# Sparse-attention layer of a two-block network: the value products of both attention branches issued together per tile of queries, and the compressed probabilities transposed at full width

## The chip, the cores and the metric

The kernel runs on one core of a Trainium2 chip. The metric is the device time of one execution in microseconds; lower is better. The engines are TensorE (PE, with its weight loads shown apart as PEld), VectorE (DVE), ScalarE (ACT), GpSimd (POOL) and the DMA queue of SyncE (SP).

## The reference, cut to what matters

The program is two two-layer blocks on 512 tokens of width 1024. Only the last mixer, the sparse attention (NSA), is touched by the change:

```
q = rope(q.reshape(B, S, 16, 64)) * 64 ** -0.5          # 4 groups of 4 heads share keys and values
kcmp, vcmp = compress(kc), compress(vc)                  # 31 compressed keys and values
block of queries:
    pc = softmax(where(valid, q @ kcmp, NEG));  o_c = pc @ vcmp
    ps = softmax(where(causal, q @ k_sel, NEG)); o_s = ps @ v_sel   # 8 blocks of 64, top 16: all are selected
    pw = softmax(where(window, q @ kwin, NEG)); o_w = pw @ vwin      # window 512 = the sequence
o = sum over the three of gates * out;  o = o * silu(z);  y = o @ w_out
```

With 512 tokens every block is selected and the window covers everything, so the second and third softmax are full causal attention with keys and values of their own.

## The kernel before, in words

The heads are worked in 8 pairs p of 2 heads j; a pair has 4 tiles t of 128 queries. One (p, t) is a *unit*; there are 32. A unit has two branches b. Branch 0 holds the compressed and the selected attention, branch 1 the window. `probs` issues the scores of one branch of a unit on TensorE (lines 1741, 1746, 1748 for b = 0, line 1752 for b = 1), takes the maximum and the exponentials on VectorE and ScalarE (lines 1757 and 1763), and multiplies the probabilities by gate and reciprocal sum on VectorE (line 1771).

`attend` goes through the units. For each branch it transposes the probabilities `p` of both heads on TensorE (line 1803), copies them on ScalarE from PSUM to a tile `at` (line 1805), and for b = 0 also transposes the compressed probabilities `pc` (line 1808) and copies them on VectorE to `pcT` (line 1809). It then issues the same branch's scores of the *next* unit (`first(u + 1, b)`) and last the value products into the accumulator `po` (line 1815 with the compressed values `vcz`, line 1818 with `vs`). A product has 64 output columns in its weights, so that head 0 writes partitions 0 to 63 and head 1 partitions 64 to 127; all other matmuls of this stage are 128 wide. A float32 product is two passes in the trace, so a pair of them (j = 0 and 1) is four rows.

The order of the work comes from two things. `attend` is a generator, and the main stream (the projections of z, of the next group's queries and keys, and then the output projection, all recorded by lines 225 to 227) calls `tick` between its matmuls; `tick` steps every generator whose due time has passed. A `yield cost, latency` sets the next due time, with `LT = LA = 0.36` and `LQ = 0`. Behind that, the build lays the instructions of each engine in an order of its own and gives the PSUM tiles `sm` (4 buffers, for scores and transposes) and the SBUF tiles their places, so the final order is seen only in the built program. `finish` multiplies the accumulator by z (line 1829) when a pair is done; the output projection waits for it.

Of the kernel before, what the change touches and what calls it, by code (L numbers as in the profile page):

```python
# [16 lines left out]
P = 128  # L17
# [4 lines left out]
LQ, LT, LA = 0.0, 0.36, 0.36  # L22
# [83 lines left out]
class Net:  # L106
# [1416 lines left out]
    def nsa_(self, x, after):  # L1523
        nc, a = self.nc, self.a
        V, G, S = nc.vector, nc.gpsimd, nc.scalar
        mm, tr = nc.tensor.matmul, nc.tensor.transpose
        ident, w = self.ident, a["nsa_w_in_2"][0]
        one = lambda shape, name, dt=F32: self.wk.tile(shape, dt, name=name, tag=name, bufs=1)
        s2 = lambda tag, bufs, shape=(P, T), dt=F32: self.t(list(shape), tag, bufs, dt)
# [54 lines left out]
        vcz = one([P, 4, 2, 64], "vcz")  # L1584
# [3 lines left out]
        m = P - 1  # L1588

        def small(i):  # L1590

            n = "kv"[i]
            tmp = s2("p", 4)
            per = tmp[:16, 384:]
            nc.sync.dma_start(per, a[f"nsa_pe_{n}_2"][0].rearrange("(i s) d -> i (s d)", s=2))
            pp = self.sm_ps()
            tr(pp[:, :16], per, ident[:16, :16])
            pe = s2("pe", 2, (P, 16))
            V.tensor_copy(pe, pp[:, :16])
            w2 = tmp[:, :256].rearrange("p (k j c) -> p k j c", k=2, j=2)  # L1600
            for j in range(2):
                nc.sync.dma_start(w2[:, :, j], a[f"nsa_c{n}_w2_2"][0].rearrange("(k p) c -> p k c", p=P))
            pes[i] = pe, w2, tmp[:, 256:]

        def prepare(i, b):

            if b == 0:
                small(i)
            while not all(by_t[i, t].done for t in range(NT)):
                yield 0.0, 0.5  # L1610
            src = flat[i].rearrange("p g c -> p (g c)")[:, 16 * b:16 * b + 16 * m]
            src = src.rearrange("p (c i e) -> p e i c", e=2, i=8)[:, 0]
            if (i, b) == (1, 0):
                hl = [s2("Q2", 4, (P, 2, T), F32R).rearrange("p j c -> p (j c)") for _ in range(2)]
            else:
                c8 = self.c8().rearrange("p (j i) c -> p j (i c)", j=2)
                hl = [c8[:, 0], c8[:, 1]]
            hl = [v.rearrange("p (i c) -> p i c", c=P)[:, :, :m] for v in hl]
            for c in range(0, 8, 4):
                raw = s2("at", 3).rearrange("p (i c) -> p i c", c=P)[:, :, :m]  # L1620
                k = 8 * b + c
                (G if i else V).tensor_tensor(raw, src[:, c:c + 4], pes[i][0][:, k:k + 4, None].to_broadcast([P, 4, m]),
                                              op=ALU.add)
                self.split(hl[0][:, c:c + 4], hl[1][:, c:c + 4], raw)
                yield 0.0, 1.2
            parts[i, b] = hl
# [94 lines left out]
        used = [Flag() for _ in range(8)]  # L1721
        pairs = [Flag() for _ in range(8)]
        pcT = [one([P, P], f"pcT{i}") for i in range(2)]
        for i in range(2):
            V.memset(pcT[i], 0.0)
        cat = [None, None]
        lhs = Operand(lambda k, s, n: [v[:, k % 4, s:s + n] for v in cat[k // 4]])
        zt = {}
# [45 lines left out]
        pp, pcs, pos = {}, {}, {}  # L1774

        def attend():
            units = [(p, t) for p in range(8) for t in range(NT)]

            def first(u, b):
                p, t = units[u]  # L1780
                if b == 0:
                    if t == 0:
                        while p // 2 not in grp or len(grp[p // 2]) < NT or not all(s.done for s in grp[p // 2].values()):
                            yield 0.0, 1.8
                    pcs[u] = s2("pc", 2, (P, 64)), s2("st", 3, (P, 2, 6))
                pp[u, b] = probs(p, b, t, *pcs[u])
                yield 0.0011 * 128 * (t + 1) + 0.3, LQ

            yield from first(0, 0)
            yield from first(0, 1)  # L1790
            yield 0.0, 0.8
            for u, (p, t) in enumerate(units):
                g = p // 2
                c = slice(t * P, (t + 1) * P)
                if t == 0:
                    pos[p] = self.mm_ps()
                po = pos[p]
                for b in range(2):
                    at = []
                    for j in range(2):  # L1800
                        pt = self.sm_ps()
                        for i in range(t + 1):
                            tr(pt[:, i * P:(i + 1) * P], pp[u, b][j][:, i * P:(i + 1) * P], ident)  # L1803
                        at.append(s2("at", 3))
                        S.copy(at[j][:, :(t + 1) * P], pt[:, :(t + 1) * P])
                    if b == 0:
                        pt = self.sm_ps()
                        tr(pt[:64, :P], pcs[u][0], ident)
                        V.tensor_copy(pcT[t % 2][:64], pt[:64, :P])
                    yield 0.22 * (t + 1), LT  # L1810
                    if u + 1 < len(units):
                        yield from first(u + 1, b)
                    if b == 0:
                        for j in range(2):
                            mm(po[j * 64:(j + 1) * 64, c], vcz[:, g, j], pcT[t % 2], start=True, stop=False)
                    for i in range(t + 1):
                        for j in range(2):
                            mm(po[j * 64:(j + 1) * 64, c], vs[g][:, i, b * 64:(b + 1) * 64],  # L1818
                               at[j][:, i * P:(i + 1) * P], start=False, stop=b == 1 and i == t)
                    yield 0.27 * (t + 1) + 0.13, LA  # L1820
                if t == NT - 1:
                    used[p].done = True
                    self.spawn(finish(p, po), 1.45)

        def finish(p, po):
            while p not in zt:
                yield 0.0, 0.5
            z = zt[p]
            V.tensor_tensor(z, z, po, op=ALU.mult)  # L1829
            if cat[p // 4] is None:  # L1830
                cat[p // 4] = (self.c8(), self.c8())
            self.split(cat[p // 4][0][:, p % 4], cat[p // 4][1][:, p % 4], z)
            pairs[p].done = True
            yield 0.0, 0.0
# [13 lines left out]

        self.lin_nat(x, w, 0, 8, [(1024, 256), (2560, 48)], ev_c(0))
        preps = [self.spawn(prepare(0, b), 2.0) for b in range(2)]  # L1850
        self.lin_nat(x, w, 0, 8, [(1280, 256)], ev_c(1))
        preps.append(self.spawn(prepare(1, 0), 2.0))
        group(0)
        compress(0, preps[:2], lambda: preps.append(self.spawn(prepare(1, 1))))
        compress(1, preps[2:])
        self.spawn(attend(), 6.0)
        for g in range(4):
            z_block(g)
# [64 lines left out]
```

## Time and profile before

| what | value |
|---|---|
| median of 3 runs | 1997.81 us (1997.23 to 1997.83) |
| the profiled execution: time, span | 1995.69 us, 1994.0 us |
| TensorE clock granted | 0.995 of full speed |
| TensorE busy | 1924.9 us, 97% of the span |
| VectorE, ScalarE, GpSimd busy | 1451.8, 1014.8, 217.0 us |
| transposes of p (line 1803) in the trace | 320, from 1675.8 to 1966.8 us |
| value products (line 1818) in the trace | 640 passes, from 1677.5 to 1968.7 us |

The units of attention run from about 1669 to 1970 us of the span. The form `128*64` in a row is a matmul with 64 columns of weights, `128*128` one with 128. In a timeline a row with `x8` is eight neighbouring instructions, with its start and the time to the last one's end. The duration of a single matmul includes its pipeline; what it costs TensorE is the step from its start to the next one's start.

### The profile page before, as it was taken

What the parts mean: (1) busy time and instruction counts of PE and PEld (TensorE: products, weight loads), DVE (VectorE), ACT (ScalarE), POOL (GpSimd) and SP (SyncE); (2) the same over time, 40 slices, a digit from 0 to 9 for tenths busy, and PEclk for the clock granted to TensorE, in tenths of its full rate; (3) what the DMA queues carried; (4) which work ended last, traced back from release to release, by engine and by line L of the source; (5) the groups of instructions that cost most, each with busy time, mean ns of one, the idle gap of its engine ahead of it and who ended that gap; (6) DMA issues with size and microseconds to landing.
All of it is one profiled execution on the core that took longest, in us unless ns stands there. A gap on an engine that the chain in (4) does not pass through costs nothing.

```text
span 1994.0 us, 29961 instructions
## 1 busy us (share of the span) xinstructions
PE 1924.9 (97%) x11221; PEld 1602.4 (80%) x11221; DVE 1451.8 (73%) x2823; ACT 1014.8 (51%) x2144; POOL 217.0 (11%) x213
## 2 busy tenths in 40 slices
PE   7989989999999999999999999999999999999997
PEld 7778769788796888877879788788888797777776
DVE  5876857887989465787878897945445687878866
ACT  4645244454465245666446365525433455666664
POOL 1121110000000031431000000000110131010100
PEclk9999999999999999999999999999999999999999
DMA  6212222334333122211422343212412235202101
GB/s 182 80 32 70 74 85 85 106 96 128 94 96 121 39 90 85 75 43 57 145 84 85 116 121 112 86 51 76 132 43 84 77 91 129 64 8 58 46 20 43
DMA packets 148066, 165.08 MB, mean 83 GB/s; under 512 B 29168, under 2 KB 105024, under 8 KB 147920
## 3 DMA queue, kind: packets, MB, share of 16 engines
q1 hardware_dynamic: 147920, 163.16, 27.5%
q8 instruction: 89, 1.46, 0.3%
q14 instruction: 57, 0.47, 0.1%
HBM read 161.03 MB, written 2.10 MB: 82 GB/s over the span
## 4 chain that ended last, share of the span: by engine, by line
PE 74%; DVE 14%; ACT 4%; POOL 3%; issue 3%; DMA 2%; SPq 0%; DVEq 0%; POOLq 0%; ACTq 0%
PE mm L225 17%; PE mm L226 17%; PE mm L227 17%; PE mm L463 5%; DVE wlo L184 3%; POOL ss L297 2%; PE mm L1818 2%; PE sm L314 2%; PE sm L1803 1%; PE sm L227 1%; PE sm L225 1%; PE sm L226 1%; DVE hn L351 1%; PE sm L1752 1%; ACT whi L183 1%
## 5 line engine op out<-in xcount | busy, mean ns | idle before, releaser
L184 DVE TENSOR_TENSOR wlo<-raw,whi 128x1024 fp32r<-128x1024 f32 (+4 forms) x223 | 267.2, 1204 | 89.0 <-ACT whi L183 85.7
L183 ACT CAST whi<-raw 128x1024 fp32r<-128x1024 f32 (+4 forms) x223 | 224.7, 1011 | 142.1 <-PE mm L226 64.7
L225 PE MATMUL mm<-whi,xh 128*128 128x512 f32 (+3 forms) x768 | 286.6, 374 | 1.2 <-ACT whi L183 1.2
L226 PE MATMUL mm<-wlo,xh 128*128 128x512 f32 (+3 forms) x768 | 276.2, 360 | 2.6 <-DVE wlo L184 2.5
L227 PE MATMUL mm<-whi,xl 128*128 128x512 f32 (+3 forms) x768 | 276.9, 361 | 1.2 <-DVE xl L319 1.2
L225 PE MATMUL mm<-whi,c 128*128 128x512 f32 (+1 forms) x536 | 219.5, 410 | 1.7 <-DVE zt L1829 0.8
L183 ACT CAST whi<-qr 128x1024 fp32r<-128x1024 f32 x108 | 112.8, 1050 | 186.5 <-PE mm L227 124.8
L227 PE MATMUL mm<-whi,c 128*128 128x512 f32 (+1 forms) x536 | 207.5, 388 | 0.0
L226 PE MATMUL mm<-wlo,c 128*128 128x512 f32 (+1 forms) x536 | 207.1, 387 | 0.3 <-DVE wlo L184 0.3
L225 PE MATMUL mm<-xh,whi 128*128 128x512 f32 (+1 forms) x480 | 172.2, 359 | 0.0
L226 PE MATMUL mm<-xl,whi 128*128 128x512 f32 (+1 forms) x480 | 167.5, 349 | 0.0
L227 PE MATMUL mm<-xh,wlo 128*128 128x512 f32 (+1 forms) x480 | 167.3, 348 | 0.0
L297 POOL TENSOR_TENSOR ss<-ss,mhalf 128x1 f32<-128x1 f32 (+2 forms) x56 | 59.7, 1065 | 981.4 <-DVE ss L296 981.0
L225 PEld LDWEIGHTS mm<-whi,xh 128*128 128x128 f32 x768 | 145.8, 190 | 23.7 <-issue 6.3
L226 PEld LDWEIGHTS mm<-wlo,xh 128*128 128x128 f32 x768 | 146.6, 191 | 20.9 <-DVE wlo L184 4.6
L227 PEld LDWEIGHTS mm<-whi,xl 128*128 128x128 f32 x768 | 145.8, 190 | 21.7 <-DVE xl L319 1.8
L184 DVE TENSOR_TENSOR wlo<-qr,whi 128x1024 fp32r<-128x1024 f32 x108 | 131.4, 1225 | 32.0 <-ACT whi L183 31.4
L225 PEld LDWEIGHTS mm<-whi,c 128*128 128x128 f32 (+1 forms) x536 | 101.0, 188 | 26.3 <-issue 5.7
L226 PEld LDWEIGHTS mm<-wlo,c 128*128 128x128 f32 (+1 forms) x536 | 101.0, 188 | 21.5 <-issue 3.8
L227 PEld LDWEIGHTS mm<-whi,c 128*128 128x128 f32 (+1 forms) x536 | 100.7, 188 | 20.4 <-DVE c L184 0.2
L225 PE MATMUL mm<-T,whi 128*128 128x256 f32 x384 | 108.8, 283 | 0.0
L227 PE MATMUL mm<-T,wlo 128*128 128x256 f32 x384 | 108.8, 283 | 0.0
(510 smaller groups left out, 4433.8 us busy)
## 6 DMA issues: line engine op xcount, KB each, us to landing
qr<-in_w_mlp SPq DMA_DIRECT2D x84, 512.0 KB, 4.1
raw<-in_w_mlp SPq DMA_DIRECT2D x44, 512.0 KB, 4.3
raw<-in_w_ple_gate SPq DMA_DIRECT2D x16, 512.0 KB, 4.1
raw<-in_w_qkv_o SPq DMA_DIRECT2D x32, 256.0 KB, 4.1
raw<-in_w_in_e SPq DMA_DIRECT2D x48, 128.0 KB, 2.9
raw<-in_nsa_w_in SPq DMA_DIRECT2D x10, 512.0 KB, 3.8
raw<-in_nsa_w_in SPq DMA_DIRECT2D x17, 256.0 KB, 3.1
raw<-in_w_in_e SPq DMA_DIRECT2D x8, 512.0 KB, 4.8
```

Source lines behind the costliest of these rows:

```text
L183: self.nc.scalar.copy(hi, src)
L184: self.nc.vector.tensor_tensor(lo, src, hi.bitcast(F32), op=ALU.subtract)
L225: mm(out, sh, mh, start=first, stop=False, **kw)
L226: mm(out, sh, ml, start=False, stop=False, **kw)
L227: mm(out, sl, mh, start=False, stop=last, **kw)
L297: self.pow = self.nc.gpsimd.tensor_tensor(ss, ss, self.mhalf[:, :n], op=ALU.pow)
L314: nc.tensor.transpose(ps[:, j * P:(j + 1) * P], src[:, (k + j) * P:(k + j + 1) * P], self.ident)
L351: nc.vector.scalar_tensor_tensor(hn, self.h[:, t, :], ss, own["g"], op0=ALU.mult, op1=ALU.mult)
L463: nc.tensor.matmul(pss[r], hops[s][:, 2 * c + k, r * P:(r + 1) * P], w[:, k], start=fresh and c == 0 and k == 0, stop=c == 1 and k == 1, s ...
L1752: mm(ps[:, :n], q, kt[2 + i][:, :n], start=i == 0, stop=i == 1)
L1803: tr(pt[:, i * P:(i + 1) * P], pp[u, b][j][:, i * P:(i + 1) * P], ident)
L1818: mm(po[j * 64:(j + 1) * 64, c], vs[g][:, i, b * 64:(b + 1) * 64], at[j][:, i * P:(i + 1) * P], start=False, stop=b == 1 and i == t)
```

## The change

The products of branch 0 are no longer issued between the two branches' transposes; they wait until both branches have been transposed, and then both branches' products stand together. This takes four `at` tiles at once, so `at` has 5 buffers instead of 3 (the tile is also a scratch of `prepare`, earlier in this layer). One `yield` per unit goes (two of `LA` become one). `pc` becomes two fixed tiles of 128 columns with zeros in the unused ones, and its transpose is 128 wide. To make room, the scratch area that the build reserves in SBUF for dynamic DMAs (`dynamic_dma_scratch_size`) is set to 1024 bytes per partition.

```diff
-                raw = s2("at", 3).rearrange("p (i c) -> p i c", c=P)[:, :, :m]
+                raw = s2("at", 5).rearrange("p (i c) -> p i c", c=P)[:, :, :m]
...
+        pcn = [one([P, P], f"pc{i}") for i in range(2)]
         for i in range(2):
             V.memset(pcT[i], 0.0)
+            V.memset(pcn[i], 0.0)
...
-                    pcs[u] = s2("pc", 2, (P, 64)), s2("st", 3, (P, 2, 6))
+                    pcs[u] = pcn[u % 2], s2("st", 3, (P, 2, 6))
...
+                at = {}
                 for b in range(2):
-                    at = []
                     for j in range(2):
                         pt = self.sm_ps()
                         for i in range(t + 1):
                             tr(pt[:, i * P:(i + 1) * P], pp[u, b][j][:, i * P:(i + 1) * P], ident)
-                        at.append(s2("at", 3))
-                        S.copy(at[j][:, :(t + 1) * P], pt[:, :(t + 1) * P])
+                        at[b, j] = s2("at", 5)
+                        S.copy(at[b, j][:, :(t + 1) * P], pt[:, :(t + 1) * P])
                     if b == 0:
                         pt = self.sm_ps()
-                        tr(pt[:64, :P], pcs[u][0], ident)
+                        tr(pt[:, :P], pcs[u][0], ident)
                         V.tensor_copy(pcT[t % 2][:64], pt[:64, :P])
                     yield 0.22 * (t + 1), LT
                     if u + 1 < len(units):
                         yield from first(u + 1, b)
-                    if b == 0:
-                        for j in range(2):
-                            mm(po[j * 64:(j + 1) * 64, c], vcz[:, g, j], pcT[t % 2], start=True, stop=False)
+                for j in range(2):
+                    mm(po[j * 64:(j + 1) * 64, c], vcz[:, g, j], pcT[t % 2], start=True, stop=False)
+                for b in range(2):
                     for i in range(t + 1):
                         for j in range(2):
                             mm(po[j * 64:(j + 1) * 64, c], vs[g][:, i, b * 64:(b + 1) * 64],
-                               at[j][:, i * P:(i + 1) * P], start=False, stop=b == 1 and i == t)
-                    yield 0.27 * (t + 1) + 0.13, LA
+                               at[b, j][:, i * P:(i + 1) * P], start=False, stop=b == 1 and i == t)
+                yield 0.54 * (t + 1) + 0.13, LA
...
-    nc = bacc.Bacc("TRN2", target_bir_lowering=False, num_devices=1)
+    nc = bacc.Bacc("TRN2", target_bir_lowering=False, num_devices=1, dynamic_dma_scratch_size=1024)
```

The lines move by 2 or 3 in the changed kernel: 1803 becomes 1805 (transposes of p), 1808 becomes 1810 (of pc), 1815 becomes 1817, 1818 becomes 1821, 1752 becomes 1754, 1748 becomes 1750.

How the built program differs is shown at three places of TensorE's queue, all of the last pair of heads.

First, the unit of tile 0. Before, its products stand in two places with 23 rows from the first to the last; the first place, behind the next unit's branch 0 scores:

```order
L1741 MATMUL sm_18104<-ksl_16730,Q_2795_16734 128x288
L1815 MATMUL mm_18075<-pcT_13811,vcz 64x128 x2
L1818 MATMUL mm_18075<-at_18078,vt_16735 64x128
L1818 MATMUL mm_18075<-at_18082,vt_16735 64x128
L225 MATMUL mm_18087<-whi_17912,c_2489_15375 128x512
```

These rows are read with the next ones: the second place, behind the branch 1 scores.

```order
L1752 MATMUL sm_18165<-kwh_16731,Q_2795_16734 128x256
L1752 MATMUL sm_18165<-kwl_16732,Q_2795_16734 128x256
L1818 MATMUL mm_18075<-at_18134,vt_16735 64x128
L1818 MATMUL mm_18075<-at_18138,vt_16735 64x128
L225 MATMUL mm_18152<-whi_18148,c_2901_17218 128x512
```

In the changed program all six products of that unit stand behind the branch 1 scores:

```order
L1754 MATMUL sm_18088<-kwh_16735,Q_2781_16738 128x256
L1754 MATMUL sm_18088<-kwl_16736,Q_2781_16738 128x256
L1817 MATMUL mm_18022<-pcT_13811,vcz 64x128 x2
L1821 MATMUL mm_18022<-at_18025,vt_16739 64x128
L1821 MATMUL mm_18022<-at_18029,vt_16739 64x128
L1821 MATMUL mm_18022<-at_18069,vt_16739 64x128
L1821 MATMUL mm_18022<-at_18073,vt_16739 64x128
L225 MATMUL mm_18104<-whi_17964,c_2471_15318 128x512
```

So two stretches of 64-wide matmuls became one here.

Second, the unit of tile 2. Before, between the next unit's branch 0 scores (line 1748) and the branch 1 transposes (line 1803) stand eight products:

```order
L1748 MATMUL sm_18301<-ksl_16730,Q_2795_16734 128x512
L1815 MATMUL mm_18075<-pcT_13811,vcz 64x128 x2
L1818 MATMUL mm_18075<-at_18277,vt_16735 64x128
L1818 MATMUL mm_18075<-at_18283,vt_16735 64x128
L1818 MATMUL mm_18075<-at_18277,vt_16735 64x128
L1818 MATMUL mm_18075<-at_18283,vt_16735 64x128
L1818 MATMUL mm_18075<-at_18277,vt_16735 64x128
L1818 MATMUL mm_18075<-at_18283,vt_16735 64x128
L1803 MATMUL sm_18326<-ident,p_18254 128x128 x3
```

In the changed program only matmuls of the output projection (lines 225 to 227) are between them, and one product of the compressed values (line 1817) stands alone between the two heads' transposes:

```order
L1750 MATMUL sm_18250<-ksl_16734,Q_2781_16738 128x512
L225 MATMUL mm_18231<-whi_18227,c_2873_17157 128x512
L1805 MATMUL sm_18267<-ident,p_18175 128x128 x3
L226 MATMUL mm_18231<-wlo_18228,c_2873_17157 128x512
L227 MATMUL mm_18231<-whi_18227,c_2874_17158 128x512
L1817 MATMUL mm_18022<-pcT_13811,vcz 64x128
L1805 MATMUL sm_18273<-ident,p_18181 128x128 x3
L1754 MATMUL sm_18282<-kwh_16735,Q_2781_16738 128x512
```

The products of branch 0 moved behind the branch 1 scores, and the build did not keep them all together: of this unit's fourteen products one went ahead alone.

Third, the last unit of all. Before, no other matmul stands between its transposes and its products:

```order
L1803 MATMUL sm_18360<-ident,p_18299 128x128 x4
L1803 MATMUL sm_18367<-ident,p_18310 128x128 x4
L1808 MATMUL sm_18374<-ident,pc_18288 64x128
L1815 MATMUL mm_18075<-pcT_13812,vcz 64x128 x2
L1818 MATMUL mm_18075<-at_18365,vt_16735 64x128
L1818 MATMUL mm_18075<-at_18372,vt_16735 64x128
```

In the changed program matmuls of the output projection are left over and stand there:

```order
L1805 MATMUL sm_18319<-ident,p_18248 128x128 x4
L1805 MATMUL sm_18326<-ident,p_18259 128x128 x4
L1810 MATMUL sm_18333<-ident,pc_13814 128x128
L225 MATMUL mm_18312<-whi_18227,c_2873_17157 128x512
L226 MATMUL mm_18312<-wlo_18228,c_2873_17157 128x512
L227 MATMUL mm_18312<-whi_18227,c_2874_17158 128x512
L1805 MATMUL sm_18339<-ident,p_18286 128x128 x4
L1805 MATMUL sm_18346<-ident,p_18292 128x128 x4
L225 MATMUL mm_18353<-whi_18221,c_2873_17157 128x512
L226 MATMUL mm_18353<-wlo_18222,c_2873_17157 128x512
L227 MATMUL mm_18353<-whi_18221,c_2874_17158 128x512
L225 MATMUL mm_18353<-whi_18221,c_2873_17157 128x512
```

The matmuls of the output projection that the main stream had spent by then before are spread between the last units' steps now.

## The prediction

> **What bounds the kernel.** I read the engine totals and the chain that ended last on the page first, then busy time by stretches of the attention stage, then who waited for whom there.
>
> ```profile
> PE 1924.9 (97%) x11221; PEld 1602.4 (80%) x11221; DVE 1451.8 (73%) x2823; ACT 1014.8 (51%) x2144; POOL 217.0 (11%) x213
> PE 74%; DVE 14%; ACT 4%; POOL 3%; issue 3%; DMA 2%; SPq 0%; DVEq 0%; POOLq 0%; ACTq 0%
> ```
>
> TensorE is busy for 97% of the span and carries 74% of the chain, so what shortens its queue, or fills a hole in it, shortens the run. The stretches (first column: from and to; then PE, PEld, DVE, ACT, POOL, clock, DMA):
>
> ```profile
> 1669.00:1970.00 301.00, 292.50 (x2041) 231.98 (x2040) 231.44 (x876) 189.06 (x618) 23.31 (x12) 1.00 0.14 36
> 1955.00:1970.00 15.00, 12.76 (x118) 9.63 (x117) 8.63 (x33) 8.85 (x25) 0.00 (x0) 1.00 0.01 2
> ```
>
> The attention stage takes 301.0 us, of which TensorE is busy for 292.5, at full clock. Its idle time is 8.5 us, and 2.2 of that lies in the last 15 us. VectorE (231) and ScalarE (189) have room. So the change can act in two ways: on the steps between matmuls inside the 292.5 us, and on the 8.5 us of holes. The holes by what ended them (us in total, times, longest):
>
> ```profile
> PE sm L1803 <- DVE p L1771: 2.3, 4, 1.2
> PE sm L1708 <- DVE pcT L1809: 1.6, 2, 0.8
> PE mm L225 <- DVE zt L1829: 0.8, 1, 0.8
> PE sm L1808 <- ACT p L1763: 0.5, 1, 0.5
> PE mm L1818 <- ACT at L1805: 0.5, 2, 0.3
> PE sm L1741 <- ACT at L1805: 0.4, 2, 0.2
> PE sm L1752 <- ACT at L1805: 0.4, 1, 0.4
> PE sm L1748 <- ACT at L1805: 0.4, 1, 0.4
> PE mm L1815 <- DVE pcT L1809: 0.4, 1, 0.4
> ```
>
> **First term: fewer switches of width.** One stretch of products (64 columns of weights) among 128-wide matmuls, seen in TensorE's timeline; the start times are what counts:
>
> ```profile
> 1910.92 0.61 PE L1818 MATMUL mm<-at,vt 128*64 128x128 f32 x8
> ...
> 1914.95 0.34 PE L1752 MATMUL sm<-kwl,Q 128*128 128x384 f32 x1
> 1915.12 0.34 PE L1752 MATMUL sm<-kwh,Q 128*128 128x384 f32 x1
> 1915.30 0.34 PE L1752 MATMUL sm<-kwl,Q 128*128 128x384 f32 x1
> 1915.57 0.66 PE L1818 MATMUL mm<-at,vt 128*64 128x128 f32 x8
> 1916.15 0.50 PE L225 MATMUL mm<-whi,c 128*128 128x512 f32 x1
> 1916.49 0.40 PE L226 MATMUL mm<-wlo,c 128*128 128x512 f32 x1
> 1916.72 0.40 PE L227 MATMUL mm<-whi,c 128*128 128x512 f32 x1
> ...
> 1958.94 0.82 PE L1818 MATMUL mm<-at,vt 128*64 128x128 f32 x12
> ```
>
> The first and the last row follow other products of the same width. They differ by four rows, that is one pair of products, and by 0.21 us: a pair costs 0.21, and each of its two passes 0.11. Now the price of a stretch. Into it: the scores step by 0.17 to 0.18, the step onto the first product is 0.27, so 0.09 more; eight rows take 0.66 behind the switch and 0.61 in the first row, where the width does not change, 0.05 more. Out of it: a single matmul of this size lasts 0.27 (the row of line 1808 below), so the last product starts at 1915.57 + 0.66 - 0.27 = 1915.96 and line 225 follows 0.19 later, where a pass takes 0.11: 0.08 more; the next step is 0.34 where the following is 0.23: 0.11 more. Sum 0.33 us for a stretch.
>
> How many go is not what the diff suggests. The diff would leave one stretch per unit, 32. In the built order I count stretches of neighbouring rows of lines 1815 and 1818 (1817 and 1821 in the changed kernel): 64 before, 48 after. The build puts other matmuls between, as in the unit of tile 2 shown above. Saved: 16 x 0.33 = 5.3 us. Some of the broken stretches have an odd number of products, so that one runs without its partner of the other head: rounding each stretch up to pairs gives 192 pairs before and 199 after, 7 x 0.21 = 1.5 us lost. Balance of the first term: -3.8 us. The stretches lie on the path, since TensorE has no hole there to take them up.
>
> **Second term: the holes.** The products of branch 0 used to stand between a unit's steps and now stand behind the branch 1 scores, so I compared in the two built orders how much TensorE work lies between each step and what it needs.
>
> Transposes to products (through the copy `at` or `pcT`): the shortest distance was a few tenths of a microsecond in the last units and is now over 1.2 us, and the copies take 0.3 to 0.6. The holes of lines 1818 and 1815 go: 0.9 us. Scores to transposes of the same probabilities: one whole chain of a 416-wide branch, from the last score matmul to the last scaled probabilities:
>
> ```profile
> 1910.37 0.35 PE L1741 MATMUL sm<-ksl,Q 128*128 128x416 f32 x1
> 1911.74 0.58 ACT L1763 ACTIVATE p<-sm,st 128x384 f32<-128x384 f32 x1 [0.20 <-DVE st L1757]
> 1912.31 0.57 ACT L1763 ACTIVATE p<-sm,st 128x384 f32<-128x384 f32 x1
> 1914.04 0.42 DVE L1771 TENSOR_SCALAR p<-p,st 128x384 f32<-128x384 f32 x1
> ```
>
> It takes 1914.46 - 1910.37 = 4.1 us. In the new order the work between, counted with the steps above, is 4.9 us or more for this width and 6.7 or more for the widest, where the last unit had about 4. Of the 2.3 us of line 1803, 1.2 is the very first unit, which does not change; 1.1 goes. The two holes of line 1708 (1.6 us) stand where the next group's transposes came straight behind the branch 0 scores; in the new order six or five products come first, and they go. The end:
>
> ```profile
> 1963.47 0.27 PE L1808 MATMUL sm<-ident,pc 128*64 128x128 f32 x1
> 1964.12 0.44 PE L1815 MATMUL mm<-pcT,vcz 128*64 128x128 f32 x4 [0.37 <-DVE pcT L1809]
> 1966.06 1.06 PE L1803 MATMUL sm<-ident,p 128*128 128x128 f32 x8 [0.60 <-DVE p L1771]
> 1967.41 1.58 PE L1818 MATMUL mm<-at,vt 128*64 128x128 f32 x16 [0.29 <-ACT at L1805]
> 1969.77 0.50 PE L225 MATMUL mm<-whi,c 128*128 128x512 f32 x1 [0.78 <-DVE zt L1829]
> ```
>
> Before, the output projection had run dry here and the last unit waits at every step. One `LA` less per unit makes attention use up fewer main matmuls; the new order has six, three and six of them between the last steps and three behind the last product (3 x 0.23 = 0.7 us against the 0.78 of line 1829: 0.7 goes). Together 0.9 + 1.1 + 1.6 + 0.7 = 4.3 us of holes go.
>
> What is late next: the branch 1 transposes now stand straight behind the next unit's branch 0 scores, where products and six main matmuls stood. Scores and transposes share four PSUM buffers; above, the first head's scores are held until 1911.74 + 0.58 = 1912.32, 1.95 us after the last score matmul. Where a transpose or the branch 1 scores need such a buffer, what covers it is 2 to 8 transposes (0.2 to 0.9 us) and usually six main matmuls (1.4). By the places that the build assigned, most get a buffer freed long before; about four units of tile 2 and a handful of others come up 0.1 to 0.5 us short. Ends for this: nothing, and 0.5 x 12 = 6 us. I take 1.2, near the lower end, because the new order mostly has the six main matmuls there. Second term: -4.3 + 1.2 = -3.1 us. While TensorE waits, the main matmuls queued behind wait too, nothing else does.
>
> **The small edits.** The transpose of `pc` at 128 columns:
>
> ```profile
> 1917.65 0.81 PE L1803 MATMUL sm<-ident,p 128*128 128x128 f32 x6
> 1918.31 0.27 PE L1808 MATMUL sm<-ident,pc 128*64 128x128 f32 x1
> 1918.34 0.48 PE L225 MATMUL mm<-whi,c 128*128 128x512 f32 x1
> 1918.65 0.39 PE L226 MATMUL mm<-wlo,c 128*128 128x512 f32 x1
> ```
>
> Six wide transposes step by (0.81 - 0.27) / 5 = 0.11; the narrow one follows after 0.66 - 5 x 0.11 = 0.11, and line 225 follows 0.03 later. No entry or exit price is seen, so widening saves nothing: 0. Its bounds are 32 x 0.03 = 1 us lost and 32 x 0.33 = 10.6 us saved (a rival below). The Trainium skill, "TensorEngine Tiling (Array Packing)", section "Key Properties", says that changing the tiling mode drains TensorE; by that rule alone the sum would take the 10.6 us as well. The products agree with it (0.33 us), this row does not: the 64-wide transpose shows no drain.
>
> Two memsets more, and the buffers of `at` in `prepare`:
>
> ```profile
> L1725 DVE MEMSET pcT<- x2: 165/165/165, 1589.5 to 1589.6; 128x128 f32 x2
> PE sm L1573 <- POOL hn L1543: 1.3, 1, 1.3
> q1 hardware_dynamic: 147920, 163.16, 27.5%
> ```
>
> The memsets cost VectorE 2 x 0.17 us; TensorE could lose 0 to 0.3, I take 0, since VectorE has its own holes around the start of the layer. In that part three matmuls (0.7 us) now precede the transposes of line 1573, which waited 1.3 us: between 0.7 saved and nothing; I take 0 for that too. GpSimd's queue swaps one addition of `prepare` with one of the rope. SyncE's queue keeps its order, the change issues no DMA, and all data moves on the queue of the last row, which the smaller scratch area does not serve: 0.
>
> **Sum.** -3.8 - 3.1 = -6.9 us. The profiled execution took 1995.69 us (span 1994.0), 2.1 below the median of the runs; the difference does not depend on the level, so 1997.8 - 6.9 = 1990.9 us. A change within 0.2% (4 us) can't be told from none here.
>
> **Rivals.** (1) *The switches are saved, the holes come back elsewhere.* For: the same chains of VectorE and ScalarE serve every unit, and their waits are several short ones. Against: the distances grew wherever the trace shows a hole. Time: 1997.8 - 3.8 = 1994.0, half of it inside the 4 us.
>
> (2) *The PSUM buffers become the bound; slower.* Place: branch 1 transposes and scores behind branch 0 scores. Price per unit: for the widest scores the transposes come directly, and by the chain above a buffer is held 1.95 us against 0.7 of covering transposes, 1.2 us; for the others up to 0.5. If the buffers came in plain rotation: 8 x 1.2 + 24 x 0.4 = 19 us, and with half of that, without the gain of the second term, 1997.8 - 3.8 + 9.6 = 2003.6. It decides from 4 + 3.8 = 7.8 us, 0.25 us per unit. Against: the assigned places, and that before, too, scores followed transposes closely without holes in most units.
>
> (3) *The narrow transpose did pay a switch that its row does not show.* 10.6 us more: 1980.3. The page named above would have it so; the start times speak against it.
>
> (4) *The build undoes it:* broken stretches with more unpaired products than I count eat the switches, the holes stay: 1997.
>
> **Chances.** Forecast 0.58 (1985 to 1993.5); rival 1 0.23 (half same, half faster); rival 2 0.11; rival 3 0.03; rival 4 0.05. Faster 0.58 + 0.11 + 0.03 = 0.72; same 0.12 + 0.05 = 0.17; slower 0.11. The low end of the range is the first term, all holes that the first unit does not cause (8.5 - 1.2 = 7.3) and the 0.7 of line 1573: 1997.8 - 11.8 = 1986, and 1 us for what the steps hide; the high end takes in rivals 1 and 4 up to 1996.5.
>
> **What would show it.** The stretches in the trace: 48, each with the same steps in and out; if the steps are smaller, the first term is wrong. The idle time of TensorE in the attention stage should fall from 8.5 to about 5.4 us, the last 15 us to under 0.5, and the waits of lines 1708, 1818 and 1829 should vanish. Waits of the transposes or scores on line 1763's exponentials (1765 there) would speak for rival 2. The step onto the wide `pc` transpose should stay 0.11. I would be wrong above all if the new adjacency makes many short waits, since I priced those from one chain.

## The result and the profile after

| | before | after |
|---|---|---|
| median of 5 runs each, same chip | 1997.83 us (1997.23 to 1999.30) | 1986.31 us (1982.84 to 1988.59) |
| ratio, 95% interval | 1 | 0.9941 (0.993 to 0.9953) |
| profiled execution, span | 1995.69, 1994.0 us | 1988.08, 1986.3 us |
| granted clock of the profiled execution | 0.995 | 0.992 |

The change saves 11.5 us; the forecast was 6.9 (1990.9 us, range 1985.0 to 1996.5). A second set of runs of both (e1) gave a ratio of 0.9932 (0.992 to 0.9945). The two profiled executions differ by only 7.6 us because the part ahead of attention, which the change does not touch, took 4.3 us longer in the one of the changed kernel, at a lower clock: the first transpose of `p` starts at 1680.1 us instead of 1675.8. So I compare the attention stage, from the start of that transpose to the end of the span: **318.2 us before, 306.2 after, 12.0 saved.**

The page's engine totals and chain of the changed kernel, and the same stretches as before (from and to; length; PE, PEld, DVE, ACT, POOL; clock, DMA):

```profile
PE 1921.3 (97%) x11221; PEld 1603.9 (81%) x11221; DVE 1444.9 (73%) x2825; ACT 1012.7 (51%) x2144; POOL 214.9 (11%) x213
PE 76%; DVE 12%; ACT 4%; POOL 3%; issue 2%; DMA 2%; SPq 0%; DVEq 0%; POOLq 0%; ACTq 0%
```

```profile
1669.00:1970.00 301.00, 297.01 (x2121) 240.75 (x2120) 231.31 (x890) 191.04 (x628) 22.04 (x12) 1.00 0.15 40
1955.00:1970.00 15.00, 15.00 (x101) 12.21 (x100) 6.92 (x13) 5.34 (x13) 0.00 (x0) 1.00 0.01 1
```

TensorE's idle time in the stage fell from 8.5 to 4.0 us, and from 2.2 to nothing in the last 15 us. What is left, by what ended it:

```profile
PE sm L1805 <- DVE Q L1712: 1.3, 2, 0.7
PE sm L1805 <- DVE p L1773: 1.2, 1, 1.2
PE sm L1805 <- DVE pcT L1811: 0.6, 1, 0.6
PE sm L1743 <- DVE pcT L1811: 0.3, 1, 0.3
PE sm L1805 <- ACT p L1765: 0.3, 1, 0.3
```

The waits of the products, of line 1708 and of line 1829 are gone from the list. New are transposes of `p` (1805) that wait for a PSUM buffer: 1.3 until VectorE has read the next group's transposed queries (`Q`, line 1712), 0.6 until it has read `pcT`, 0.3 until ScalarE has read scores. The 1.2 is the very first unit's, as before. TensorE's timeline around one joined stretch:

```profile
1934.91 0.28 PE L1754 MATMUL sm<-kwl,Q 128*128 128x256 f32 x1
1935.12 0.44 PE L1817 MATMUL mm<-pcT,vcz 128*64 128x128 f32 x4
1935.39 0.61 PE L1821 MATMUL mm<-at,vt 128*64 128x128 f32 x8
1935.92 0.50 PE L225 MATMUL mm<-whi,c 128*128 128x512 f32 x1
1936.26 0.39 PE L226 MATMUL mm<-wlo,c 128*128 128x512 f32 x1
1936.49 0.40 PE L227 MATMUL mm<-whi,c 128*128 128x512 f32 x1
```

The unit's 12 passes now pay once: 0.21 onto the first where the scores step by 0.11 to 0.12, and 0.34 from the first main matmul to the second where the next step is 0.23, the same price as before.

**How switches and waits were separated.** Idle time counts only what the modelled ends of the matmuls leave open. So for every trace I took the steps from one matmul's start to the next one's, between the first transpose of `p` and the end. A step's usual value is the lower third (30th percentile) among all fourteen traces of the steps with the same widths of the matmul before, this one and the next, where a product counts as a width of its own; inside a stretch of products it is the lower third of the stretches with the same number of rows. The sum of the usual values holds the switches; what lies above it is waiting. Both sums end at the start of the last matmul; the 8.7 us behind it are the same in all kernels and stand in the column of the stage alone. This gives, for the kernels below (all in us, but for counts; the stage is the attention stage as above; the ratio is to the kernel before on the same chip):

| kernel | median | ratio (95%) | stage | stretches / pairs | usual steps | waits | VectorE lengthened |
|---|---|---|---|---|---|---|---|
| before | 1997.83 | 1 | 318.2 | 64 / 192 | 292.3 | 17.2 | 10.2 |
| after | 1986.31 | 0.9941 (0.993 to 0.9953) | 306.2 | 48 / 199 | 288.9 | 8.6 | 1.3 |
| e1 after, again | 1984.95 | 0.9932 (0.992 to 0.9945) | 306.1 | 48 / 199 | 288.9 | 8.5 | 1.3 |
| e2 merged, two turns | 1987.47 | 0.9945 (0.9932 to 0.9959) | 309.2 | 49 / 202 | 289.6 | 10.9 | 8.2 |
| e3 split, one turn | 1990.17 | 0.9957 (0.9945 to 0.997) | 310.1 | 70 / 197 | 294.6 | 6.8 | 1.3 |
| e4 compressed apart | 1994.66 | 0.9985 (0.9976 to 0.9994) | 315.3 | 81 / 201 | 299.4 | 7.2 | 1.6 |
| e5 split, other turn | 1996.12 | 0.9986 (0.9978 to 0.9995) | 315.8 | 68 / 195 | 295.3 | 11.9 | 2.3 |
| e6 fewest stretches | 1982.23 | 0.9923 (0.9911 to 0.9936) | 304.3 | 39 / 197 | 283.8 | 11.8 | 7.7 |
| e7 longer turn | 1989.13 | 0.9963 (0.995 to 0.9975) | 310.0 | 41 / 195 | 285.8 | 15.5 | 7.6 |
| e8 narrow `pc` | 1985.81 | 0.9942 (0.9929 to 0.9956) | 306.1 | 48 / 199 | 288.9 | 8.5 | 1.3 |
| e9 e7, shared buffer | 1992.98 | 0.9981 (0.9972 to 0.999) | 314.0 | 40 / 195 | 286.5 | 18.8 | 7.6 |
| e10 after, shared buffer | 1989.91 | 0.9964 (0.9951 to 0.9976) | 310.8 | 46 / 198 | 289.1 | 13.0 | 1.3 |
| e11 e6, shared buffer | 1986.50 | 0.9949 (0.9936 to 0.9961) | 306.9 | 38 / 197 | 284.5 | 13.7 | 6.8 |
| e12 wide `pc` alone | 1998.96 | 1.0007 (0.9998 to 1.0016) | 318.3 | 64 / 192 | 292.3 | 17.4 | 10.2 |

(The last column is explained after e7.) By this, the 12.0 us of the change are **3.4 of switches and 8.6 of waits.** A straight fit of the usual steps over the eleven different orders (after, e1 and e8 are one, as are before and e12) gives 0.32 us for a stretch and 0.17 for a pair, the latter with a standard error of 0.11; it misses single orders by up to 1.7 us.

Before, 2.0 of the 17.2 us of waits stand inside five stretches of products, where a list of idle times hardly shows them. Four of these have 16 rows; such a stretch, a usual one, and ScalarE's copies beside the first:

```profile
1748.26 1.58 PE L1818 MATMUL mm<-at,vt 128*64 128x128 f32 x16
1937.51 1.09 PE L1818 MATMUL mm<-at,vt 128*64 128x128 f32 x16
1747.63 1.06 ACT L1805 COPY at<-sm 128x512 f32<-128x512 f32 x2
```

The second copy ends at 1748.69 and a row of that stretch starts at 1748.75, 0.33 us after the one before it, where no step of a usual stretch is over 0.16: the second head's products wait for their copy. In the changed kernel no stretch is lengthened.

### The profile page after: what moved, and what is told of

Same layout as the page of the kernel before. It is cut to its first block, busy times and chain, and to the rows that moved or that the text cites. A ratio compares the mean times of both kernels' runs of the same rounds, so it can differ in the third digit from the quotient of the medians.

```text
span 1986.3 us, 29961 instructions
## 1 busy us (share of the span) xinstructions
PE 1921.3 (97%) x11221; PEld 1603.9 (81%) x11221; DVE 1444.9 (73%) x2825; ACT 1012.7 (51%) x2144; POOL 214.9 (11%) x213
## 4 chain that ended last, share of the span: by engine, by line
PE 76%; DVE 12%; ACT 4%; POOL 3%; issue 2%; DMA 2%; SPq 0%; DVEq 0%; POOLq 0%; ACTq 0%
PE mm L225 18%; PE mm L227 18%; PE mm L226 18%; PE mm L463 5%; DVE wlo L184 2%; POOL ss L297 2%; PE mm L1821 2%; PE sm L1805 2%; PE sm L314 2%; PE sm L227 1%; PE sm L225 1%; PE sm L226 1%; PE sm L1754 1%; DVE hn L351 1%; ACT whi L183 1%
## 5 line engine op out<-in xcount | busy, mean ns | idle before, releaser
L225 PE MATMUL mm<-T,whi 128*128 128x256 f32 x384 | 108.7, 283 | 0.0
L226 PE MATMUL mm<-T,whi 128*128 128x256 f32 x384 | 108.7, 283 | 0.0
```

The source lines that it names most:

```text
L225: mm(out, sh, mh, start=first, stop=False, **kw)
L226: mm(out, sh, ml, start=False, stop=False, **kw)
```

## The experiments

Two theories stood first. Theory 1: the gain is the forecast's two terms, fewer switches and, from the new order of the steps, longer distances. Theory 2: the waits went because `attend` hands the main stream one turn less per unit (a turn is a `yield` with a latency, in which main matmuls are let in), which is a side effect of the one dropped `yield`.

**e1: the changed kernel again.** No edit.

> The changed kernel, a second time, on the chip of the next three kernels. All theories: 1986.3 us (0.9941 of before) within 1.5 us. What is open is its level in the stretch before attention: the profiled run of it stood 3.1 us behind the kernel before in the MLP (943 to 1289 us of the span), where nothing was changed. If that is a run-to-run difference it is under 1 us here; if it comes from the shifted SBUF addresses it is 3 us again.

1984.95 us, stage 306.1: the stage repeats within 0.1 us. The profiled run again reached attention late (1680.5 us) and again at clock 0.992, but e8, with the same smaller scratch area, reached it at 1675.7 at clock 0.994. So the later start goes with the clock and not with the moved addresses.

**e2: merged products, both turns.** The changed kernel with

```diff
                     if u + 1 < len(units):
                         yield from first(u + 1, b)
+                    if b == 0:
+                        yield 0.27 * (t + 1) + 0.13, LA
...
-                yield 0.54 * (t + 1) + 0.13, LA
+                yield 0.27 * (t + 1) + 0.13, LA
```

> The changed kernel, but with the turn for the main stream (the yield with LA) kept in each branch, as before the change. Built order: 49 stretches of products instead of 48 (64 before), 202 pairs instead of 199 (192 before), and 69 main matmuls behind the last product as before. Theory 1 (order: switches at 0.33 us, and the longer distances between a step and what it needs): switches 15 x 0.33 - 10 x 0.21 = -2.8 us, and most of the 7.6 us by which the waits fell stays away, all but about 1 us at the end of the stage: -9.4, 1988.4 us. Theory 2 (the dropped turn fills the holes): only the switches are left, -2.8, 1995.0 us, and the idle time of TensorE in the attention stage is back at 8 us.

1987.47 us, near theory 1's 1988.4; theory 2's 1995.0 is out. Switches: 289.6 against 292.3, 2.7 less, of the 2.8 expected. Waits: 17.2 to 10.9, so 6.3 of the 8.6 stay away, where theory 1 wanted all but 1 us. The merge alone brings the switches and a good part of the waits.

**e3: the products where they were, one turn less.** The kernel before with

```diff
-                    yield 0.27 * (t + 1) + 0.13, LA
+                    yield 0.27 * (t + 1) + 0.13, LA if b else 0.0
```

> The kernel before with nothing changed but the turn: no LA behind branch 0's products (a yield with latency 0). Built order: 70 stretches, 197 pairs. Theory 1 (switches and distances): 6 x 0.33 + 5 x 0.21 = +3.0 us, the holes stay or get a little worse: 2000.8 us. Theory 2 (the dropped turn fills the holes): +3.0 - 7.6 = -4.6, 1993.2 us.

1990.17 us: theory 1 is 10.6 too high, theory 2 is nearer, 3.0 too high. With *more* stretches than before (70, usual steps 2.3 higher, of the 3.0 expected) it saves 8.1 us of stage: waits fall from 17.2 to 6.8, lower than in the changed kernel. The waits of this kernel, TensorE, whole stage:

```profile
PE sm L1803 <- DVE p L1771: 1.2, 1, 1.2
PE sm L1741 <- DVE pcT L1809: 1.2, 1, 1.2
PE mm L225 <- DVE zt L1829: 0.8, 1, 0.8
PE sm L1752 <- DVE Q L1712: 0.3, 1, 0.3
```

One new wait of 1.2 on line 1741; the first unit's 1.2 and the end's 0.8 stay; the many short ones are gone. So the two parts of the change overlap: **only the merge takes away switches, but each of the two takes away waits**, the merge alone 6.3 us, the dropped turn alone 10.4, and both together 8.6, slightly less than the dropped turn alone.

**e4: the compressed products apart again.** The changed kernel with

```diff
+                    if b == 0:
+                        for j in range(2):
+                            mm(po[j * 64:(j + 1) * 64, c], vcz[:, g, j], pcT[t % 2], start=True, stop=False)
...
-                for j in range(2):
-                    mm(po[j * 64:(j + 1) * 64, c], vcz[:, g, j], pcT[t % 2], start=True, stop=False)
```

> The changed kernel, but with the compressed products issued right behind the next unit's branch 0 scores and only the other products together at the end. Built order: 81 stretches instead of 48, 201 pairs instead of 199; turns and wide transposes as in the changed kernel. Theory 1 (a stretch costs 0.33 us): 33 x 0.33 + 2 x 0.21 = +11.3 us over the changed kernel, 1997.6 us, and the holes stay filled. Rival (a stretch costs less than its steps show, and the gain was all in the waits): under +4 us, below 1990.5 us.

1994.66 us, 9.7 over e1 on the same chip, of the 11.3 expected; the rival (under 4) is out. Usual steps rise by 10.5 us for 33 stretches and 2 pairs, 0.31 to 0.32 for a stretch; waits are 1.3 lower. A stretch costs what its steps show.

**e5: the other turn dropped.** If the turns use up the main matmuls too early, so that later steps find none to stand behind (before, 95, 74, 56 and 56 attention matmuls in a row had no main matmul between them), then any turn dropped helps. The kernel before with

```diff
-                    yield 0.22 * (t + 1), LT
+                    yield 0.22 * (t + 1), LT if b else 0.0
```

> The kernel before, but the turn that goes is the one behind branch 0's transposes (LT), and the one behind branch 0's products stays. Built order: 68 stretches, 195 pairs, longest runs of attention matmuls without a main matmul 25, 24, 24, 24 (before 95, 74, 56, 56; one turn less behind the products 30, 30, 26, 24). Theory S (supply: each turn uses up main matmuls, three turns per unit use them up too early, and the waits stand where none is left): any turn dropped helps alike; waits -6.3 to -8.4 us, stretches +1: 1990.5 us. Theory P (place: a turn behind transposes covers the copies that follow, one behind products covers nothing): this is the wrong turn to drop, the waits stay or grow: 1998 us or more.

1996.12 us: between the two. The long runs are gone, but waits fall only to 11.9. Its waits:

```profile
PE mm L1815 <- DVE pcT L1809: 1.2, 3, 0.5
PE sm L1741 <- DVE pcT L1809: 0.9, 2, 0.4
...
PE sm L1808 <- ACT p L1763: 0.7, 1, 0.7
```

Products wait for `pcT`, and the branch 0 scores for buffers, which the dropped turn's main matmuls used to cover: by the steps, scores of branch 0 wait 5.1 us (3.2 before, 1.6 in e3). So it matters which turn goes. The reading that fits is theory P's: main matmuls behind the transposes cover the copies, those behind the products of branch 0 do not. But theory P had the waits stay or grow, and they fell by 5.3 us; what took those away no run shows.

**e6: fewest stretches.** The changed kernel with `LQ, LT, LA = 0.36, 0.36, 0.0`.

> The changed kernel with other latencies (LQ 0.36, LA 0): turns behind scores and transposes, none behind products. Built order: 39 stretches and 197 pairs (changed kernel 48 and 199), but runs of 84, 64, 64, 47 attention matmuls without a main matmul (changed kernel 35, 24, 22, 22). Theory S (switches and the supply of main matmuls both count): switches 9 x 0.33 = -3.0, waits back by 2.5 (as in the kernel with two turns) to 6.7 us (as before): 1985.5 to 1989.7 us, slower than the changed kernel although it has the fewest switches. Rival (the switches are what counts): 1986 - 3 = 1983 us.

1982.23 us, the fastest of all kernels run: nearer the rival (1983) than theory S. Against the changed kernel usual steps fall by 5.1 us (9 stretches and 2 pairs are 3.4, 0.5 is two matmuls missing from this trace, whose time then counts as waiting, and 1.2 is not explained) and waits rise by 3.2, inside what theory S had said. Runs of 84 and 64 attention matmuls without a main matmul did not bring the waits back to 17. As a gain over the changed kernel take the 1.8 us of the stage; the two sets of runs are from different chips.

**e7: a longer turn.** The changed kernel with `LT` 0.65.

> The changed kernel with LT 0.65 instead of 0.36: the built order has 41 stretches and 195 pairs instead of 48 and 199, and runs without a main matmul of 33, 33, 30, 24, near those of the changed kernel. Both theories: 7 x 0.33 = -2.3 us, 1983.5 us; it is the candidate for a version faster than both.

A miss: 1989.13 us instead of 1983.5. The switches went as expected (usual steps 3.1 lower), but waits are back at 15.5, although no run without a main matmul is over 33. Theory S falls: the length of such runs does not tell the waits. The waits, and the work around the largest, on all engines:

```profile
PE sm L1805 <- ACT p L1765: 3.2, 3, 1.4
PE sm L1810 <- ACT p L1765: 1.3, 2, 0.6
```

```profile
1789.32 1.93 POOL L1543 TENSOR_TENSOR hn<-ra,rb 128x768 f32<-128x768 f32 x1 [9.73 <-DVE rb L1542]
1789.48 1.82 DVE L1773 TENSOR_SCALAR pc<-pc,st 128x32 f32<-128x32 f32 x1
...
1791.21 0.34 DVE L1773 TENSOR_SCALAR p<-p,st 128x256 f32<-128x256 f32 x1
...
1792.04 0.43 DVE L1759 CUSTOM_DVE_ANT_0 sm<-sm,late 128x256 f32<-128x256 f32 x1
...
1793.08 0.47 ACT L1765 ACTIVATE p<-sm,st 128x256 f32<-128x256 f32 x1
...
1793.24 0.44 PE L1805 MATMUL sm<-ident,p 128*128 128x128 f32 x2 [1.43 <-ACT p L1765]
```

The transpose waits for a PSUM buffer until ScalarE has read the scores; that reading is late because VectorE's maximum is late; and that is late because a scaling of 32 columns, ahead of it in VectorE's queue, took 1.82 us beside GpSimd's rope addition (line 1543). Over before, after and e2 to e7, the 7 scalings of `pc` that start while such an addition runs took 1.81 to 1.82 us; the 505 others have a median of 0.24 and none is over 0.25. Of operations that read PSUM, the 18 copies to `pcT` and the 23 subtractions for `Q` (line 1712) that start beside one are not longer (0.28 and 0.43 us, as elsewhere). Grouped by line, VectorE's scalings of `pc`, of before, after and e7 in turn (behind the first bar us in total, mean ns of one):

```profile
L1771 DVE TENSOR_SCALAR pc<-pc,st 128x32 f32<-128x32 f32 x64 | 18.4, 287 | 0.6
```

```profile
L1773 DVE TENSOR_SCALAR pc<-pc,st 128x32 f32<-128x32 f32 x64 | 15.2, 238 | 0.7
```

```profile
L1773 DVE TENSOR_SCALAR pc<-pc,st 128x32 f32<-128x32 f32 x64 | 21.4, 335 | 0.7
```

The last column of the table sums this for VectorE's operations in the stage that ran beside a GpSimd addition and more than 0.3 us over the median of their shape. It mostly goes with the waits: 10.2 and 17.2 before, 1.3 and 8.6 after, 7.6 and 15.5 in e7, 1.3 and 6.8 in e3; the exceptions are e5, which lost its cover, and e10 below, whose waits come from a shared buffer. How much of the waits it can explain shows in where they stand. Of TensorE's waits, those that end while a lengthened operation runs or within 2 us behind it are 3.3 of 17.2 us before, 0.1 of 8.6 after, 0.4 of 6.8 in e3 and 5.7 of 15.5 in e7. So it can account for most of what e7 lost against the changed kernel (5.6 of 6.9 us), but for only some 3 of the 8.6 us that the change saved; with 6 us in place of 2 it is 6.1 and 3.1. The twelve additions are the same in all kernels; what the order changes is which of VectorE's operations they fall on. The Trainium skill, "SBUF — State Buffer", section "Who interferes with whom", says that VectorE and GpSimd share one pair of SBUF ports, that whichever takes it first holds it for a whole instruction, and that scalings and additions of two SBUF inputs can need it; the trace agrees in which operations stretch, and in that the copies from PSUM do not. No run moved the additions by themselves, so this part is read from the traces, not shown by an experiment.

**e8: the narrow transpose in the changed kernel**, and **e12: the wide one in the kernel before.** e8 goes back to

```diff
-                    pcs[u] = pcn[u % 2], s2("st", 3, (P, 2, 6))
+                    pcs[u] = s2("pc", 2, (P, 64)), s2("st", 3, (P, 2, 6))
...
-                        tr(pt[:, :P], pcs[u][0], ident)
+                        tr(pt[:64, :P], pcs[u][0], ident)
```

and e12 makes the opposite edit in the kernel before, with the smaller scratch area.

> The changed kernel with the compressed probabilities transposed 64 wide as before; the built order is the changed kernel's in all else (48 stretches, 199 pairs). Theory 1 (a 64-wide transpose pays no switch, its step is 0.11 us in and 0.03 out like the wide one's): 1986 us, as the changed kernel, within 1 us. Rival (it pays one like the products): 32 x 0.33 = +10.6, 1996.6 us.

> The kernel before with the two small edits alone: pc in fixed tiles of 128 columns, transposed in full width, and the scratch area of 1024 bytes. Built order: 64 stretches, 192 pairs, as before. Theory 1 (the narrow transpose pays no switch, the moved SBUF addresses nothing): 1998 us, within 1 us of before. Rival (it pays one, 0.33 us each): 1987.4 us.

1985.81 and 1998.96 us: no effect either way (e12's ratio includes 1; the stages are 306.1 and 318.3, within 0.15 of after and before). TensorE in the same unit, narrow in e8, then wide in the changed kernel:

```profile
1906.77 0.82 PE L1803 MATMUL sm<-ident,p 128*128 128x128 f32 x6
1907.42 0.27 PE L1808 MATMUL sm<-ident,pc 128*64 128x128 f32 x1
1907.45 0.48 PE L225 MATMUL mm<-whi,c 128*128 128x512 f32 x1
```

```profile
1911.25 0.82 PE L1805 MATMUL sm<-ident,p 128*128 128x128 f32 x6
1911.90 0.27 PE L1810 MATMUL sm<-ident,pc 128*128 128x128 f32 x1
1911.93 0.48 PE L225 MATMUL mm<-whi,c 128*128 128x512 f32 x1
```

The steps are equal to the hundredth. The rule of the Trainium skill, "TensorEngine Tiling (Array Packing)", section "Key Properties", that a change of the tiling mode drains TensorE, agrees with the products' 0.33 us and not with this transpose.

**e9, e10, e11: one PSUM buffer less per unit.** The last attempt was to take waits for buffers away, in e7, the changed kernel and e6: for tiles 0 to 2 `pc` is transposed into the free columns of head 1's buffer,

```diff
-                        pt = self.sm_ps()
-                        tr(pt[:, :P], pcs[u][0], ident)
-                        V.tensor_copy(pcT[t % 2][:64], pt[:64, :P])
+                        o = (t + 1) * P
+                        if t == NT - 1:
+                            pt, o = self.sm_ps(), 0
+                        tr(pt[:, o:o + P], pcs[u][0], ident)
+                        V.tensor_copy(pcT[t % 2][:64], pt[:64, o:o + P])
```

> The kernel of e7 (LT 0.65) with one PSUM buffer less used per unit: for tiles 0 to 2 the transposed pc goes into the free columns of the buffer that holds head 1's transposed p. Built order: 40 stretches and 195 pairs (e7 41 and 195), else nearly the same. In e7's trace 4.5 us of waits of transposes (3.2 on p, 1.3 on pc) end with ScalarE's exponentials of line 1765. Theory B (the transposes wait for a PSUM buffer that the scores still hold): half or more of that goes, 2.3 to 4.5 us, and 0.3 for the stretch: 1984.3 to 1986.5 us. Theory C (the transposes wait for their probabilities, the buffers do nothing): 1988.8 us, as e7.

> The changed kernel with the same sharing of a PSUM buffer. Built order: 46 stretches, 198 pairs (changed kernel 48 and 199), nothing else far. Theory B: of the 3.3 us of waits at its p transposes 2.0 are not the first unit's; 0 to 2.2 us go, and 0.7 for the stretches: 1983 to 1985.2 us. Theory C: 1985.3 us.

> The kernel of e6 (fewest stretches) with the same sharing. Built order: 38 stretches, 197 pairs (e6 39 and 197). Theory B: waits fall by up to 1.5 us and 0.3 for the stretch: 1980.4 to 1981.9 us, the fastest version. Theory C: 1981.9 us.

Missed in all three: 1992.98, 1989.91 and 1986.50 us, each some 4 us slower than its kernel without the sharing (by the stage 3.9, 4.7 and 2.6). The waits of e9:

```profile
PE sm L1812 <- ACT at L1807: 4.6, 8, 1.1
PE sm L1805 <- ACT p L1765: 3.1, 3, 1.4
```

The transposes of `pc` (line 1812 there) now wait until ScalarE has copied head 1's probabilities out of the buffer they share, a wait that my edit made and that I had not priced: by the steps 6.8 us in e9 (1.8 in e7), 5.1 in e10 (none in the changed kernel), 3.8 in e11 (0.5 in e6). The waits that e9 was to take away stayed, 3.1 of 3.2, as theory C had it; but a rotation with one buffer less to take is not more buffers, so whether a fifth buffer would remove them stays open.

## Why the prediction was right, and where its sizes were off

**Switches: −3.8 forecast, −3.4 measured.** The count (48), the steps in and out and the price of 0.33 all came out; the fit over eleven orders gives 0.32. The +1.5 us for odd stretches holds as well. I had priced a product without its partner at a whole pair, and in the changed kernel a stretch with such a product, six rows, takes 0.65 us, where eight rows take 0.66 in a row of the prediction:

```profile
1731.49 0.65 PE L1821 MATMUL mm<-at,vt 128*64 128x128 f32 x6
```

**Holes: −3.1 forecast; −4.5 by idle time, −8.6 by the steps.** This is the term whose size was wrong. The single steps, each with what the steps in the trace show (waits over 60 ns only, before to after):

- Products (lines 1815 and 1818): forecast −0.9, measured 3.5 to 0. Right in kind, but idle time shows only a quarter of it; 2.0 us stood inside the stretches.
- Line 1708: forecast −1.6, measured 2.1 to 0.2. Right in size, incomplete in cause: before, VectorE's scalings ahead of the copy to `pcT` had run beside GpSimd's addition:

```profile
1796.82 2.24 DVE L1771 TENSOR_SCALAR p<-p,st 128x256 f32<-128x256 f32 x2
1797.07 1.83 POOL L1543 TENSOR_TENSOR hn<-ra,rb 128x768 f32<-128x768 f32 x1 [6.32 <-DVE rb L1542]
1798.97 0.27 DVE L1809 COPY pcT<-sm 64x128 f32<-64x128 f32 x1
1799.30 0.66 PE L1708 MATMUL sm<-ident,hn 128*128 128x128 f32 x4 [0.80 <-DVE pcT L1809]
```

  The two scalings of a pair of heads took 2.24 us, where the median of one is 0.35. It was not only that products were missing ahead of line 1708.
- The end (line 1829): forecast −0.7, measured 0.85 to 0.11. Right, from the three more main matmuls behind the last product. e2, with both turns and 69 main matmuls there, has this wait back at 0.86.
- Transposes of `p`: forecast 1.1 gone and 1.2 new. Measured 2.1 to 3.3: the new buffer waits came, 1.3 + 0.6 + 0.3 = 2.2 by idle time, most of them behind `Q` and `pcT`, which I had not named. The price was 1 us low.
- Scores of both branches: not in the sum at all. Their waits fell from 5.3 to 2.2 us, 28 and 14 waits of up to 0.6. The list of holes had shown only the largest of them (lines 1741, 1752, 1748), and I let them stand. This is the biggest miss, 3 us. The wait of line 1808, 0.5 in the list and 0.7 by the steps, was not in the sum either and went.

So the forecast of 6.9 fell short of 12.0 by 5.5 us of waits, less 0.4 of switches. The reason I gave for the second term, the longer distances that the merge makes, is only a part: e2 shows that the merge alone takes away 6.3 us of waits, e3 that the dropped turn alone takes away 10.4, and the forecast had used the turn for the 0.7 at the end alone.

That the time fell inside the range is in part luck. Its low end of 1985.0 counted on the waits that idle time shows, 8.5 us, while the steps held 17.2, of which half went; 1986.31 lies 1.3 us above that end, and the second set of runs (e1, 1984.95) just below it.

**The rivals.** Rival 1 (holes come back) did not happen here, but it is what e7 is. Rival 2 (PSUM buffers) happened at a tenth of its price, 2.2 of 19 us; e7 shows how near it lay, with 4.5 us of transposes waiting for scores to be read. Rival 3 is out by e8 and e12. Rival 4 did not happen.

## What to carry to other kernels

Where TensorE is the bound, count waits from start to start, against the usual step of the same neighbours: idle time showed 8.5 us where the steps held 17.2, and the difference lay in many short waits, and in waits inside stretches of like matmuls. Take the usual time for those stretches too, or the waits in them pass for the price of the work. When a change merges work and drops a point where other work is let in, try each alone; here the merge alone was worth 9.0 us of the stage (e2), the dropped turn alone 8.1 (e3), and together they gave 12.0. Two latencies changed afterwards (e6, e7) moved the time by 1.8 us down or 3.9 up in the stage, so the order after such an edit is worth a small search on the chip.

## What the runs showed of the hardware

A VectorE scaling of 32 columns can take 1.8 us instead of 0.24, without any wait shown, when GpSimd is in the middle of an addition: the trace shows it as a long duration, and TensorE's wait names ScalarE two steps later. Stretches of 64-wide products cost 0.32 to 0.33 us to enter and leave, a single 64-wide transpose nothing, and a product without its partner in the other half as much as a pair (0.65 us for six rows, 0.66 for eight). And the time of one kernel follows the granted clock closely: 25 runs of the kernel before at 0.994 average 1997.5 us, 12 at 0.995 average 1996.3, 12 at 0.993 average 2000.0 (over three chips); a comparison to 2 us needs either several runs or the stage alone.
